# Stick-breaking attention layer: values projected for two pairs of heads with the tokens on the partitions

## The chip, the cores and the metric

The kernel runs on one core of one Trainium2 chip. The metric is the device time of one execution in microseconds, from the first to the last instruction of the program and what lies around them.

## The reference

One layer of a trunk with stick-breaking attention: 2048 tokens, model width 1024, 16 heads of 64, then a SwiGLU feed-forward with 2816 hidden channels. All is float32; the kernel splits operands of most products into a high and a low part and adds three products.

```python
h = modulate(rms_norm(x, norm_g[0]), sh_m, sc_m)
q, k, v = (h @ w_qkv) split, 16 heads of 64
z = q @ k.T / 8                       # per head, keys before the query only
rest = reversed cumulative sum over keys of softplus(z)
a = exp(z - rest)
y = (a @ v) @ w_o
x = x + gt_m * rms_norm(y, norm_g[1])
h = modulate(rms_norm(x, norm_g[2]), sh_f, sc_f)
x = x + gt_f * rms_norm((silu(g) * u) @ w_out, norm_g[3])      # g, u = h @ w_in
```

## The kernel before, in words

**Stages.** First the norm and the modulation of the tokens (four blocks of 512, b = 0 to 3), then attention with the projections woven in, then the output projection (tiles y), the feed-forward (tiles s, then o<-b,ol). The TensorE, ScalarE, VectorE and GpSimd queues run in the order in which the program was written; the order on SP, which issues every transfer, is set by the scheduler. A transfer waits on one of eight semaphores that are used in turn, so at most eight are under way.

**Projections.** Heads go in pairs, p = 0 to 7. A step (p, b) of `project` makes keys, queries and values of one pair for one block of tokens; the steps (0, 0) and (1, 0) are made at the start, in `products`. A product is 8 slices, one for each 128 input channels; a slice is three matmuls of 128x512 (`mm3`, L196 to L198) with the weights stationary and the tokens moving. All three products, t = 1 (keys), 0 (queries) and 2 (values), come out with channels on the partitions. Keys and queries are split into two parts (`split`, L499, L500) and taken by DMA into kt and qt. Values are copied to vT by ScalarE (L539), and after two empty slices (`VGAP`) turned by four transposes of 128x128 into the bank vt (L545), from where ScalarE (L549) and VectorE (L550) write the two parts of the tile v. A step is 3 x 8 + 2 = 26 slices. Normalised tokens are kept in DRAM as h_s and come back for each step in four tiles ht of 1 MB; there are five buffers of ht.

**Attention.** A unit is (p, head e, query block qb, key block sc); it has four slots, one for each 128 queries. In a slot the program writes: scores z (two matmuls, L597), two sigmoids on ScalarE (L614, L616), a scan on VectorE (L631, or L626 on the diagonal), a product on GpSimd (L638), four transposes t (L648), the split of t into aT (ScalarE L658, VectorE L664), and the product with the values o (two matmuls, L676). Later stages belong to earlier slots: transposes are five or six slots behind the scores, products with values nine. Pair p has 80 slots: 8, 16, 24 and 32 for its query blocks 0 to 3.

**The order around the change.** In each slot `project_to` writes projection slices up to a number that grows by a constant rate with the slots done:

```python
AHEAD = 3 * KC + 6
RATE = (sum(SLICES) - AHEAD) / (NPAIR * (48 + 32 * DIAG_WEIGHT) - 24 - 8 * DIAG_WEIGHT)
project_to(AHEAD - max(0, EAGER - 1 - s) + weight * RATE)
```

which is 1.343 slices a slot (a slot on the diagonal counts 0.8). Ahead of a block's first score `project_to` writes whatever its step still lacks. When all 780 slices are written, the first part of the output projection (`lead_in`: L1092 and L1100 on VectorE, then `out_projection`) fills the slots of the last query block.

Of the kernel before, what the change touches and what calls it, by code (L numbers as in the profile page):

```python
# [41 lines left out]
SLICES = [0, 0] + [3 * KC + VGAP] * (NPAIR * NB - 2)  # L42


AHEAD = 3 * KC + 6
DIAG_WEIGHT = 0.8
RATE = (sum(SLICES) - AHEAD) / (NPAIR * (48 + 32 * DIAG_WEIGHT) - 24 - 8 * DIAG_WEIGHT)
# [4 lines left out]
    "ht": 5, "whl": 4, "qt": 3, "kt": 7, "v": 7, "aT": 4, "qkn": 2, "wraw": 2,  # L52
# [40 lines left out]
    2: [(0, 6), (2, 0), (2, 2), (2, 4), (2, 6)],  # L93
    3: [(0, 4), (0, 7), (2, 2), (2, 4), (2, 6)],
# [10 lines left out]
PLACES = [("ht", 64), ("qt", 0), ("v", 0), ("kt", 0), ("whl", 0), ("aT", 0), ("wraw", 0), ("qkn", 0), ("tmp", 0), ("a", 0)]  # L105
# [19 lines left out]
def hybrid_trunk_kernel(  # L125
# [12 lines left out]
    wqkv: bass.AP,  # L138
# [32 lines left out]
    v_park = dram.tile([P, 4, 2, 2, HD], F32, name="v_park")  # L171
# [266 lines left out]
    waiting = []  # L438

    def unpark():  # L440
# [14 lines left out]
        nc.sync.dma_start(f32(v), v_park)  # L455
        keys[p, b], queries[p, b], values[p, b] = kt, qt, v

    def project(at):
# [10 lines left out]
        def product(t):  # L469
            if begun:  # L470
                if at == 0 and t != 2:
                    first_norm(1, 2 + (t == 0))
# [4 lines left out]
            for k in range(KC):
                if t == 1:
                    if p == 0:
                        first_norm(b, NORM_IN_KEYS[b].get(k, KC))  # L480
                    if k in (3, 5) and waiting:
                        waiting.pop(0)()
# [4 lines left out]
                if ahead and k == 0:  # L487
                    load_weights(p + 1, t)
                if ahead and k == 6:
                    split_weights(p + 1, t)  # L490
                mm3(acc, (w[0][:, k], w[1][:, k]), (h[k][:, 0], h[k][:, 1]), k == 0, k == KC - 1)
# [49 lines left out]
        def values_turn():  # L541
            pool, ptag = (zps, "z") if early else (accps, "acc")
            pt = pool.tile([P, 4, 2, HD], F32, name=f"vt{p}_{b}", tag=ptag)
            for i in range(4):
# [3 lines left out]
            v = att.tile([P, 4, 2, 2, HD], F32R, name=f"v{p}_{b}", tag="v", bufs=BUFS["v"])  # L548
            nc.scalar.copy(v[:, :, :, 0], pt)  # L549
            nc.vector.tensor_tensor(v[:, :, :, 1], pt, f32(v[:, :, :, 0]), op=ALU.subtract)  # L550
            if parked:
                nc.sync.dma_start(v_park, f32(v))
            else:
                values[p, b] = v

        if early:
            waiting.append(values_turn)
            return
        for _ in range(VGAP):
            yield  # L560
        values_turn()
# [1229 lines left out]
```

## Time and profile before

| what | value |
|---|---|
| time, median of 3 runs | 2834.68 us (2834.43 to 2834.89) |
| span of the profiled execution | 2832.3 us |
| TensorE (PE) busy | 2795.9 us, 99% |
| VectorE (DVE) busy | 2032.2 us, 72% |
| ScalarE (ACT) busy | 1631.9 us, 58% |
| GpSimd (POOL) busy | 1270.2 us, 45% |
| mean granted clock of TensorE | 0.997 |
| moved by DMA | 521 MB, mean 184 GB/s |

No other time of the profiled execution is given than its span; the median of the runs is 2.4 us above it. Busy time of TensorE counts matmuls that overlap, so that a busy share of 99% doesn't mean the engine at its peak: what a matmul costs is the distance from its start to the next one's.

### The profile page before, as it was taken

The numbers are of one execution on the slowest core, as the hardware profiler recorded it, in microseconds if no ns is written. First come the engines' busy times: TensorE is split into PE (matmuls) and PEld (weight loads), VectorE is DVE, ScalarE is ACT, GpSimd is POOL, SyncE is SP. The second block draws the span as 40 slices with busy tenths as digits, with TensorE's granted clock in tenths as the row PEclk, the third lists the DMA queues.
The fourth block names the chain that finished last, engine by engine and source line by source line (L and its number), as shares of the span: only waits on it lengthen the run. The fifth ranks groups of instructions, "written<-read, shape, count | busy, mean of one in ns | idle before, by whom it ended". The sixth has DMA issues, their size and how long they took to land.

```text
span 2832.3 us, 41825 instructions
## 1 busy us (share of the span) xinstructions
PE 2795.9 (99%) x13817; PEld 2333.2 (82%) x13817; DVE 2032.2 (72%) x2847; ACT 1631.9 (58%) x3277; POOL 1270.2 (45%) x2024
## 2 busy tenths in 40 slices
PE   9899999999999999999999999999999999999998
PEld 7688888888888888887888888888888888888887
DVE  7788888889889888889866766555785665133376
ACT  6787778788777878777655533333433333322243
POOL 1565666666566655656410222221222222544454
PEclk9999999999999999999999999999999999999999
DMA  9874556656665644556289644334463335545575
GB/s 374 303 217 152 187 168 215 223 184 218 198 202 199 205 129 162 194 156 209 95 297 312 203 140 151 123 99 159 133 188 100 110 108 164 192 141 154 181 226 188
DMA packets 240652, 521.06 MB, mean 184 GB/s; under 512 B 22577, under 2 KB 108593, under 8 KB 223538
## 3 DMA queue, kind: packets, MB, share of 16 engines
q1 hardware_dynamic: 240434, 518.38, 56.4%
q8 instruction: 109, 1.79, 0.3%
q14 instruction: 109, 0.89, 0.1%
HBM read 351.04 MB, written 118.49 MB: 166 GB/s over the span
## 4 chain that ended last, share of the span: by engine, by line
PE 89%; DVE 5%; DMA 2%; ACT 2%; issue 1%; SPq 0%; POOL 0%; DVEq 0%; POOLq 0%; ACTq 0%
PE s L196 10%; PE s L198 10%; PE s L197 10%; PE z L597 8%; PE o L676 8%; PE t L648 8%; PE pj L196 5%; PE pj L198 5%; PE pj L197 5%; PE o L196 5%; PE o L197 5%; PE o L198 5%; PE y L198 1%; PE y L196 1%; PE y L197 1%
## 5 line engine op out<-in xcount | busy, mean ns | idle before, releaser
L638 POOL TENSOR_TENSOR a<-a,w 128x512 f32<-128x512 f32 (+3 forms) x640 | 621.9, 972 | 222.2 <-DVE w L631 133.5
L631 DVE TENSOR_TENSOR_SCAN w<-z,c,begin 128x512 f32<-128x512 f32 x384 | 488.9, 1278 | 80.9 <-ACT z L616 61.2
L196 PE MATMUL s<-r,l 128*128 128x512 f32 x1232 | 481.5, 391 | 0.9 <-ACT p L1466 0.8
L198 PE MATMUL s<-r,l 128*128 128x512 f32 x1232 | 479.8, 389 | 0.0
L197 PE MATMUL s<-r,l 128*128 128x512 f32 x1232 | 479.6, 389 | 0.0
L614 ACT ACTIVATE a<-z 128x512 f32<-128x512 f32 (+3 forms) x640 | 346.9, 542 | 165.0 <-PE z L597 131.8
L676 PE MATMUL o<-aT,v 128*128 128x512 f32 (+3 forms) x1280 | 384.8, 382 | 0.0
L664 DVE TENSOR_TENSOR aT<-t,aT 128x512 fp32r<-128x512 f32 (+3 forms) x640 | 359.2, 595 | 23.1 <-ACT aT L658 22.7
L597 PE MATMUL z<-kt,qt 128*128 128x512 f32 (+3 forms) x1280 | 364.1, 366 | 1.7 <-DVE w L626 1.7
L658 ACT CAST aT<-t 128x512 fp32r<-128x512 f32 (+3 forms) x640 | 314.3, 533 | 74.8 <-PE t L648 64.7
L616 ACT ACTIVATE z<-z 128x512 f32<-128x512 f32 (+3 forms) x640 | 345.2, 539 | 0.0
L1530 POOL TENSOR_TENSOR one<-p,p 128x512 f32<-128x512 f32 x44 | 70.9, 1612 | 574.0 <-issue 303.6
L648 PE MATMUL t<-begin,a 128*128 128x128 f32 x2176 | 296.0, 274 | 17.9 <-DVE aT L664 17.0
L648 PEld LDWEIGHTS t<-begin,a 128*128 128x128 f32 x2176 | 255.5, 141 | 68.5 <-DVE aT L664 20.4
L196 PE MATMUL pj<-ht,w 128*128 128x512 f32 x768 | 308.6, 402 | 0.0
L198 PE MATMUL pj<-ht,w 128*128 128x512 f32 x768 | 302.8, 394 | 0.0
L197 PE MATMUL pj<-ht,w 128*128 128x512 f32 x768 | 302.1, 393 | 0.3 <-DVE ht L397 0.3
L196 PEld LDWEIGHTS s<-r,l 128*128 128x128 f32 x1232 | 231.3, 188 | 50.4 <-ACT p L1466 1.7
L198 PEld LDWEIGHTS s<-r,l 128*128 128x128 f32 x1232 | 231.3, 188 | 48.3 <-DVE l L1384 0.4
L197 PEld LDWEIGHTS s<-r,l 128*128 128x128 f32 x1232 | 231.3, 188 | 48.2 <-issue 0.5
L597 PEld LDWEIGHTS z<-kt,qt 128*128 128x128 f32 x1280 | 230.8, 189 | 39.6 <-DVE w L626 2.3
L626 DVE TENSOR_TENSOR_SCAN w<-z,begin 128x128 f32<-128x128 f32 (+3 forms) x256 | 208.6, 818 | 70.7 <-ACT z L616 58.0
(180 smaller groups left out, 4869.8 us busy)
## 6 DMA issues: line engine op xcount, KB each, us to landing
ht<-h_s SPq DMA_DIRECT2D x108, 1024.0 KB, 8.1
wi<-in_win SPq DMA_DIRECT2D x86, 512.0 KB, 4.0
qt<-qn SPq DMA_DIRECT2D x124, 256.0 KB, 4.8
ol_qt<-act_s SPq DMA_DIRECT2D x56, 512.0 KB, 3.6
act_s<-S SPq DMA_DIRECT2D x66, 256.0 KB, 4.1
br<-in_wout SPq DMA_DIRECT2D x66, 256.0 KB, 3.5
h_s<-ht SPq DMA_DIRECT2D x16, 1024.0 KB, 11.1
o_s<-os SPq DMA_DIRECT2D x128, 128.0 KB, 2.6
```

What stands on the lines that cost most here:

```text
L196: nc.tensor.matmul(acc, lhs[0], rhs[0], start=first, stop=False, **kw)
L197: nc.tensor.matmul(acc, lhs[0], rhs[1], start=False, stop=False, **kw)
L198: nc.tensor.matmul(acc, lhs[1], rhs[0], start=False, stop=last, **kw)
L597: nc.tensor.matmul(z[:, :n], q[:, e, part, r * P : (r + 1) * P], k[:, e, :n], start=part == 0, stop=part == 1,)
L614: nc.scalar.activation(a[:, :n], z[:, :n], AF.Sigmoid, scale=QK_SCALE)
L616: nc.scalar.activation(z[:, :n], z[:, :n], AF.Sigmoid, scale=-QK_SCALE)
L631: nc.vector.tensor_tensor_scan(rest[:, rev], left[:, rev], begin[:, :BT][:, rev], initial=carries[r], op0=ALU.mult, op1=ALU.bypass,)
L638: nc.gpsimd.tensor_tensor(a[:, :n], a[:, :n], rest[:, 1 : n + 1], op=ALU.mult)
L648: nc.tensor.transpose(pt[:, rb * P : (rb + 1) * P], weighed[i, rb][:, j * P : (j + 1) * P], ident)
L658: nc.scalar.copy(hl[:, 0, t0:], pt[:, t0:])
L664: nc.vector.tensor_tensor(hl[:, 1, t0:], pt[:, t0:], f32(hl[:, 0, t0:]), op=ALU.subtract)
L676: nc.tensor.matmul(acc[:, t0:], lhs, hl[:, part, t0:], start=sc == qb and j == 0 and part == 0, stop=sc == 0 and j == 3 and part == 1,)
```

## The change

Values of two pairs of heads (a group) are projected at once, and the other way round: a slice of the values is six matmuls of 128x256 (`value_product`) with 128 tokens stationary and 256 value channels moving, for two of the four runs of 128 tokens in a block. So a product of values, 8 slices, is half a block of tokens for two pairs, and comes out with tokens on the partitions; vT, vt and their transposes are gone. The two parts are written by ScalarE and VectorE to a tile vn, stored to DRAM as v_s, two transfers a product, and loaded as v by one transfer of 512 KB at the end of each step. Group g (pairs 2g and 2g + 1) is projected in the steps of pair 2g - 1 (first half of the tokens) and 2g (second half); pair 0 makes both halves of group 0, and pair 7 makes no values. A step has thus 34 slices for pair 0 (and for (2, 0)), 26 for pairs 1 to 6, 18 for pair 7; the sum is 780 as before. The buffers whl (4) become wkq (2) and wv (2). The pace is no longer constant: `pace` follows the upper hull of what each block needs, plus two slices, so that it falls in steps.

```diff
+def value_halves(p, b):
+    if p == NPAIR - 1 or (p, b) == PARKED:
+        return []
+    if p == 0 or (p, b) == (2, PARKED[1]):
+        return [0, 1]
+    return [p % 2 ^ 1]
+def value_group(p):
+    return (p + 1) // 2
+def slices_of(p, b):
+    return 2 * KC + KC * len(value_halves(p, b)) + VGAP
-AHEAD = 3 * KC + 6
+AHEAD = 4 * KC + 6
-RATE = (sum(SLICES) - AHEAD) / (NPAIR * (48 + 32 * DIAG_WEIGHT) - 24 - 8 * DIAG_WEIGHT)
+MARGIN = 2
+def needs():
+    weight = 0.0
+    for p in range(NPAIR):
+        for b in range(NB):
+            at = STEPS.index((p, b)) if (p, b) != PARKED else STEPS.index((p, 1)) - 1
+            yield weight, sum(SLICES[: at + 1]) + 1 + MARGIN
+            weight += 8 * (b + DIAG_WEIGHT)
...
-    "ht": 5, "whl": 4, "qt": 3, "kt": 7, "v": 7, "aT": 4, "qkn": 2, "wraw": 2,
+    "ht": 5, "wkq": 2, "wv": 2, "qt": 3, "kt": 7, "v": 7, "aT": 4, "qkn": 2, "wraw": 2,
...
-    2: [(0, 6), (2, 0), (2, 2), (2, 4), (2, 6)],
-    3: [(0, 4), (0, 7), (2, 2), (2, 4), (2, 6)],
+    2: [(0, 6), (2, 2), (3, 2), (3, 4), (3, 6)],
+    3: [(0, 4), (0, 7), (3, 2), (3, 4), (3, 6)],
...
+    def value_product(acc, g, h, half, k):
+        for i in range(2):
+            ts = slice((2 * half + i) * P, (2 * half + i + 1) * P)
+            mm3(
+                acc[:, i * 2 * P : (i + 1) * 2 * P], (h[k][:, 0, ts], h[k][:, 1, ts]),
+                weights["v", g, k], k == 0 and i == 0, k == KC - 1, skip_group_check=True,
+            )
...
-        acc = yield from product(2)
-        tag = "w" if early else "tmp"
-        vT = att.tile([P, BT], F32, name=f"vT{p}_{b}", tag=tag, bufs=BUFS[tag])
-        nc.scalar.copy(vT, acc)
...
-                nc.tensor.transpose(
-                    pt[:, i].rearrange("p e d -> p (e d)"), vT[:, i * P : (i + 1) * P], ident
...
-            nc.scalar.copy(v[:, :, :, 0], pt)
-            nc.vector.tensor_tensor(v[:, :, :, 1], pt, f32(v[:, :, :, 0]), op=ALU.subtract)
...
+        for half in halves_of_v:
+            acc = yield from product(2 + half)
+            acc = acc.rearrange("p (n d) -> p n d", d=HD)
+            vn = att.tile([P, 2, 2, 2, 2, HD], F32R, name=f"vn{p}_{b}_{half}", tag="qkn", bufs=BUFS["qkn"])
+            to = vn.rearrange("p i q e a d -> p (i q e) a d")
+            nc.scalar.copy(to[:, :, 0], acc)
+            nc.vector.tensor_tensor(to[:, :, 1], acc, f32(to[:, :, 0]), op=ALU.subtract)
+            for pair in range(2):
+                nc.sync.dma_start(
+                    v_s[2 * value_group(p) + pair, b][:, 2 * half : 2 * half + 2], f32(vn[:, :, pair])
+                )
         for _ in range(VGAP):
             yield
-        values_turn()
+        v = att.tile([P, 4, 2, 2, HD], F32R, name=f"v{p}_{b}", tag="v", bufs=BUFS["v"])
+        nc.sync.dma_start(f32(v), v_s[p, b])
+        values[p, b] = v
...
-                project_to(AHEAD - max(0, EAGER - 1 - s) + weight * RATE)
+                project_to(pace(weight) - max(0, EAGER - 1 - s))
```

In the first two steps the values are made by `products`, eight times four groups of three matmuls of 128x256, and `take_first_values` splits them in eight small copies and eight small subtractions; those of (1, 0) are stored, as before. The weights of the values of a group come in two halves, loaded and split in the steps around the change of pair.

Three places show the order. On TensorE, in step (3, 1), before: the end of the values. The names are z and o for scores and products with values, vt for the turned values, pj for projections.

```order
L676 MATMUL o2_0_3_6784<-aT55_0_7054,v2_0_4255 128x512 x2
L597 MATMUL z57_1_7106<-kt2_2_4993,qt2_3_5748 128x512 x2
L545 MATMUL vt3_1_7109<-begin_62,vT3_1_7062 128x128 x4
L196 MATMUL pj3_2_1_7125<-ht3_2_0_7117,w3_1_5525 128x512
L197 MATMUL pj3_2_1_7125<-ht3_2_0_7117,w3_1_5525 128x512
L198 MATMUL pj3_2_1_7125<-ht3_2_0_7117,w3_1_5525 128x512
```

And now, the first slice of the values of that step:

```order
L782 MATMUL o2_0_3_7276<-aT54_2_7491,v2_1_5456 128x512 x2
L703 MATMUL z56_3_7551<-kt2_3_6227,qt2_3_6395 128x512 x2
L248 MATMUL pj3_1_2_7562<-wv2_0_6649,ht3_1_0_7217 128x256
L249 MATMUL pj3_1_2_7562<-wv2_0_6649,ht3_1_0_7217 128x256
L250 MATMUL pj3_1_2_7562<-wv2_0_6649,ht3_1_0_7217 128x256
L248 MATMUL pj3_1_2_7562<-wv2_0_6649,ht3_1_0_7217 128x256
L249 MATMUL pj3_1_2_7562<-wv2_0_6649,ht3_1_0_7217 128x256
L250 MATMUL pj3_1_2_7562<-wv2_0_6649,ht3_1_0_7217 128x256
```

A slice of the values has six matmuls of half the width, and the four transposes at the end of a step are gone.

On TensorE in pair 7, query block 2 (unit 148), between the scores of two slots, before:

```order
L597 MATMUL z148_1_16933<-kt7_0_15238,qt7_2_16542 128x512 x2
L196 MATMUL pj7_3_1_16692<-ht7_3_3_16686,w7_1_14641 128x512
L197 MATMUL pj7_3_1_16692<-ht7_3_3_16686,w7_1_14641 128x512
L198 MATMUL pj7_3_1_16692<-ht7_3_3_16686,w7_1_14641 128x512
L196 MATMUL pj7_3_0_16949<-ht7_3_0_16680,w7_0_14806 128x512
L197 MATMUL pj7_3_0_16949<-ht7_3_0_16680,w7_0_14806 128x512
L198 MATMUL pj7_3_0_16949<-ht7_3_0_16680,w7_0_14806 128x512
L676 MATMUL o7_0_2_16930<-aT146_1_16891,v7_2_16677 128x384 x2
L597 MATMUL z148_2_16968<-kt7_0_15238,qt7_2_16542 128x512 x2
```

and now:

```order
L703 MATMUL z148_1_17684<-kt7_0_16139,qt7_2_17306 128x512 x2
L248 MATMUL pj7_3_0_17638<-ht7_3_1_17357,w7_0_15708 128x512
L249 MATMUL pj7_3_0_17638<-ht7_3_1_17357,w7_0_15708 128x512
L250 MATMUL pj7_3_0_17638<-ht7_3_1_17357,w7_0_15708 128x512
L782 MATMUL o7_0_2_17681<-aT146_1_17642,v7_2_17353 128x384 x2
L703 MATMUL z148_2_17705<-kt7_0_16139,qt7_2_17306 128x512 x2
```

One slice stands here in place of two. Counted over the whole order, the slices between the first score of one query block and that of the next are, for block 2 and 3 of pair 6 and blocks 0, 1 and 2 of pair 7: before 28, 38, 7, 22, 23; now 24, 28, 6, 14, 12. Ahead of the first score of all they were 66 and are 74; in blocks 0 to 3 of pair 0 they were 15, 21, 29, 37 and are 17, 24, 32, 41.

On SP, around the loads of ht for step (3, 3), before:

```order
L229 DMA aw3_0_6_7661<-in_ada_w 128x1024
L532 DMA qt3_2_7451<-qn3_2_7448 64x1024 x4
L415 DMA ht3_3_1_7678<-h_s3_86 128x2048
L415 DMA ht3_3_2_7680<-h_s3_86 128x2048
L415 DMA ht3_3_3_7682<-h_s3_86 128x2048
L684 DMA o_s3_90<-os2_1_3_7617 64x512 x2
```

and now:

```order
L629 DMA qt3_2_8140<-qn3_2_8137 64x1024 x4
L1245 DMA wo_s0_121<-wos0_5_8125 128x1024
L790 DMA o_s0_117<-os3_0_0_8259 64x512 x2
L1238 DMA wor0_6_8360<-in_wo 128x512
L493 DMA ht3_3_1_8375<-h_s3_116 128x2048
L644 DMA v_s4_2_99<-vn3_2_0_8320 128x2x256
L644 DMA v_s5_2_103<-vn3_2_0_8320 128x2x256
L790 DMA o_s0_117<-os3_1_0_8364 64x512 x2
L493 DMA ht3_3_2_8377<-h_s3_116 128x2048
L493 DMA ht3_3_3_8379<-h_s3_116 128x2048
```

The last two tiles of tokens now stand behind the stores of the values (which wait for VectorE) and behind a store of o that waits for ScalarE.

## Rows read from the trace of the kernel before

**Rows 1.** The page: span, and busy time of each engine.
```profile
span 2832.3 us, 41825 instructions
PE 2795.9 (99%) x13817; PEld 2333.2 (82%) x13817; DVE 2032.2 (72%) x2847; ACT 1631.9 (58%) x3277; POOL 1270.2 (45%) x2024
```
**Rows 2.** The page: the chain that ended last, by engine.
```profile
PE 89%; DVE 5%; DMA 2%; ACT 2%; issue 1%; SPq 0%; POOL 0%; DVEq 0%; POOLq 0%; ACTq 0%
```
**Rows 3.** Busy time by stretch, cut at first scores of blocks named in the prediction.
```profile
core 0: us, PE busy (x) PEld busy (x) DVE busy (x) ACT busy (x) POOL busy (x), PEclk, DMA share, GB/s
77.60:99.00 21.40, 19.09 (x97) 15.46 (x96) 15.11 (x30) 15.12 (x32) 7.26 (x17) 0.92 0.99 343
99.00:141.10 42.10, 35.33 (x183) 28.72 (x182) 33.10 (x42) 31.81 (x70) 27.98 (x47) 0.96 0.73 262
141.10:1110.80 969.70, 964.24 (x5326) 819.00 (x5325) 837.90 (x1089) 766.61 (x1616) 619.69 (x1285) 1.00 0.60 192
...
1110.80:1158.40 47.60, 47.60 (x265) 40.65 (x263) 40.80 (x54) 40.04 (x83) 35.07 (x68) 1.00 0.60 204
1158.40:1225.20 66.80, 66.74 (x364) 56.45 (x363) 56.71 (x70) 51.21 (x104) 38.47 (x89) 1.00 0.39 115
1225.20:1240.30 15.10, 15.10 (x90) 13.01 (x89) 12.15 (x18) 11.05 (x27) 6.82 (x18) 1.00 0.79 299
1240.30:1274.70 34.40, 33.01 (x181) 27.76 (x180) 30.20 (x41) 26.05 (x58) 18.50 (x41) 1.00 0.53 146
1274.70:1321.60 46.90, 44.74 (x250) 37.76 (x248) 41.58 (x55) 36.92 (x79) 27.93 (x62) 1.00 0.73 244
1321.60:1383.70 62.10, 59.40 (x328) 49.96 (x328) 57.93 (x73) 51.07 (x108) 38.88 (x87) 1.00 0.16 58
```
**Rows 4.** Timeline of TensorE, end of the program: start us, length us, instruction.
```profile
2811.68 0.39 PE L197 MATMUL o<-b,ol_qt 128*128 128x512 f32 x1
...
2816.44 0.39 PE L197 MATMUL o<-b,ol_aT 128*128 128x512 f32 x1
2816.67 0.39 PE L198 MATMUL o<-b,ol_aT 128*128 128x512 f32 x1
2816.90 0.28 PE L196 MATMUL o<-b,ol_qt 128*128 128x256 f32 x1
2817.01 0.28 PE L197 MATMUL o<-b,ol_qt 128*128 128x256 f32 x1
2817.13 0.28 PE L198 MATMUL o<-b,ol_qt 128*128 128x256 f32 x1
2817.25 0.28 PE L196 MATMUL o<-b,ol_qt 128*128 128x256 f32 x1
```
**Rows 5.** Timeline of TensorE in attention: two scores of 256 columns.
```profile
101.85 0.40 PE L597 MATMUL z<-kt,qt 128*128 128x256 f32 x2
102.08 0.40 PE L196 MATMUL pj<-ht,w 128*128 128x512 f32 x1
```
**Rows 6.** Timeline of TensorE: the transposes of one step's values.
```profile
600.09 0.60 PE L545 MATMUL vt<-begin,vT 128*128 128x128 f32 x4
600.45 0.48 PE L196 MATMUL pj<-ht,w 128*128 128x512 f32 x1
600.76 0.39 PE L197 MATMUL pj<-ht,w 128*128 128x512 f32 x1
```
**Rows 7.** Groups by line, attention: busy us, mean ns, idle before and its releaser.
```profile
L545 PE MATMUL vt<-begin,vT 128*128 128x128 f32 x128 | 19.4, 274 | 0.9 <-ACT vT L539 0.9
...
L539 ACT COPY vT<-pj 128x512 f32<-128x512 f32 x32 | 19.1, 596 | 6.5 <-PE pj L198 6.0 <-ACT z L616 0.4
```
**Rows 8.** Timelines of VectorE, TensorE and SP around the loads of xc.
```profile
106.25 1.85 DVE L384 SCALAR_TENSOR_TENSOR xc<-xc,g_eff,xv 128x512 f32<-128x512 f32 x1 [3.87 <-DMA xc<-in_xt]
...
109.90 0.55 PE L648 MATMUL t<-begin,a 128*128 128x128 f32 x3 [3.75 <-DVE aT L664]
...
94.92 2.44 SPq L331 DMA_DIRECT2D xc<-in_xt  x4
```
**Rows 9.** DMA issues: KB each, median us from issue to landing.
```profile
ht<-h_s SPq DMA_DIRECT2D x108, 1024.0 KB, 8.1
...
v_park<-v SPq DMA_DIRECT2D x1, 512.0 KB, 11.0
```

More of the change, by code (lines that the diff above doesn't have):

```diff
@@ L170, in hybrid_trunk_kernel @@
     k_park = dram.tile([P, 2, BT], F32, name="k_park")
-    v_park = dram.tile([P, 4, 2, 2, HD], F32, name="v_park")
+    v_s = {
+        (p, b): dram.tile([P, 4, 2, 2, HD], F32, name=f"v_s{p}_{b}")
+        for p in range(NPAIR) for b in range(NB) if (p, b) != EARLY[0]
+    }
     h_s = [dram.tile([P, KC, 2, BT], F32, name=f"h_s{b}") for b in range(NB)]
@@ L486, in product @@
                     first_norm(nb, NORM_AT[nb].index((t, k)))
[L487 to L491, printed above, removed]
+                ready_weights(t, k)
+                if t < 2:
+                    w = weights[p, t]
+                    mm3(acc, (w[0][:, k], w[1][:, k]), (h[k][:, 0], h[k][:, 1]), k == 0, k == KC - 1)
+                else:
+                    value_product(acc, value_group(p), h, t - 2, k)
                 slice_at[0] = k
@@ L559, in project, with take_first_values @@
         for _ in range(VGAP):
             yield
-        values_turn()
+        v = att.tile([P, 4, 2, 2, HD], F32R, name=f"v{p}_{b}", tag="v", bufs=BUFS["v"])
+        nc.sync.dma_start(f32(v), v_s[p, b])
+        values[p, b] = v
+    def take_first_values(half):
+        acc = first_acc["v", half].rearrange("p (i q e d) -> p i q e d", q=2, e=2, d=HD)
+        for pair in range(2):
+            if half == 0:
+                first_v.append(
+                    att.tile([P, 4, 2, 2, HD], F32R, name=f"v{pair}_0", tag="v", bufs=BUFS["v"])
+                )
+            to = first_v[pair][:, 2 * half : 2 * half + 2]
+            for i in range(2):
+                nc.scalar.copy(to[:, i, :, 0], acc[:, i, pair])
+                nc.vector.tensor_tensor(to[:, i, :, 1], acc[:, i, pair], f32(to[:, i, :, 0]), op=ALU.subtract)
+        if half == 1:
+            values[EARLY[0]] = first_v[0]
+            nc.sync.dma_start(v_s[PARKED], f32(first_v[1]))
@@ L762, in weights_low, with products @@
             nc.vector.tensor_tensor(lo[:, ks], raw[:, ks], f32(hi[:, ks]), op=ALU.subtract)
-    def products(p, m, *ts):
-        for t in ts or (1, 0, 2):
+    value_split = {}
+    def products(p, m):
+        for t in (1, 0):
             w = weights[p, t]
@@ L770, in products @@
             )
+        if p == 1:
+            for half in range(2):
+                value_product(first_acc["v", half], 0, first_h, half, m)
     def turn_x(m):
@@ L817, in hybrid_trunk_kernel @@
     x_load(0, 3)
-    pairs = [[(p, t) for t in (1, 0, 2)] for p in range(2)]
+    pairs = [[(0, 1), (0, 0)], [(1, 1), (1, 0), "v"]]
     row_load(0)
@@ L855, in hybrid_trunk_kernel @@
     row_done(0)
-    first_acc = {(0, t): accps.tile([P, BT], F32, name=f"pj0_0_{t}", tag="acc") for t in (1, 0, 2)}
+    first_acc = {
+        of: accps.tile([P, BT], F32, name=f"pj0_0_{n}", tag="acc")
+        for n, of in enumerate([(0, 1), (0, 0), ("v", 0)])
+    }
     weights_high(0, *pairs[0])
@@ L874, in hybrid_trunk_kernel @@
     high(1)
-    for t in (1, 0, 2):
-        first_acc[1, t] = zps.tile([P, BT], F32, name=f"pj1_0_{t}", tag="z")
+    for n, of in enumerate([(1, 1), (1, 0), ("v", 1)]):
+        first_acc[of] = zps.tile([P, BT], F32, name=f"pj1_0_{n}", tag="z")
     products(1, 0)
@@ L1373, in left_split @@
         if j == 0:
-            tag = "whl" if (n, pair) == (0, 0) else "ht"
+            tag = "wv" if (n, pair) == (0, 0) else "ht"
             left_pair[n, pair] = att.tile(
```

144 lines of the change are left out of this document (98 added, 46 removed).

## The prediction

> **What bounds the kernel now.** I read the page first. TensorE is busy for 99% of the span and every other engine for 72% or less [rows 1], and 89% of the chain that ended last is TensorE [rows 2]. So a matmul taken away should pay in full, wherever nothing else is close behind. Whether something is close is read from the stretches [rows 3], which I cut at the first score of query blocks: 77.6 is the first score of all, 99.0 and 141.1 those of blocks 1 and 2 of pair 0; 1110.8, 1158.4, 1225.2, 1240.3, 1274.7 and 1321.6 are blocks 2 and 3 of pair 6 and 0, 1, 2, 3 of pair 7; 1383.7 is the last score. The reader is to see three things. From 141.1 to 1110.8 TensorE idles for 5.5 us in 970. At the start it idles for 2.3 us of 21.4 and 6.8 us of 42.1, at a granted clock of 0.92 and 0.96. At the end VectorE is nearly as busy as TensorE: 30.2 against 33.0 us in block 1 of pair 7, 41.6 against 44.7 in block 2, and 57.9 of 62.1 (93%, its highest share in these rows) in block 3.
>
> The median of the runs is 2834.7 us, 2.4 above the profiled span; I add the terms to the median, as if the 2.4 us stayed.
>
> **Values the other way round: -4.1 us.** The change takes away 32 x 24 = 768 matmuls of 512 columns and adds 1536 of 256. Back to back, with a weight load for each, 512 columns start 0.227 us apart (22 starts from 2811.68 to 2816.67) and 256 columns 0.12 apart (three starts from 2816.90 to 2817.25) [rows 4]. So 174.3 us become 184.3: +10.0. Taken away are also 128 transposes. Four of them and one matmul of 512 lie between 600.09 and 600.76 [rows 6]: 0.67 - 0.227 = 0.44, or 0.11 each: -14.1 in all. Two scores of 256 columns between other matmuls took 0.23 together [rows 5]; with 0.115 each the term would be -11.8, and that is its other end. I take the first, since its rows have the same form, three products in a run.
>
> The Trainium skill, page TensorE: Matmul & The Clock Gate, section Back-to-back issue gap, gives a matmul alone N/2.4 + 2.5 ns, by which splitting one in two would cost 2.5 ns; an estimate from that page is +1.9 in place of +10.0. The rows show 13 ns a split, and the measurement decides.
>
> **Copies: nothing, but cover.** 32 copies vT of 0.6 us leave ScalarE [rows 7]; the subtractions on VectorE stay 32. ScalarE isn't the bound, so this is worth no more than TensorE's waits: 0.9 us before vt [rows 7] and part of the 5.5 us idle in the long stretch. The pace there rises from 1.343 to 1.383 slices a slot, which gives the other engines 3% more time. I take -2, between 0 and -5.
>
> **Slices moved to the start: -3.** Eight more slices stand ahead of the first score, and 2 and 3 more in blocks 0 and 1. TensorE has no room ahead of the first score, so the eight are paid there. In blocks 0 and 1 the added 5 x 0.68 = 3.4 us can lie in its 9.1 us of waits, and shorter waits may spare a fall of the clock: a granted share of 0.92 in 21.4 us, and of 0.96 in 42.1, is 1.7 us lost in each. That bounds the gain by -7. Against it stands the longest wait there. VectorE waits 3.87 us for xc, whose loads were issued at 94.9, and TensorE waits 3.75 us behind it [rows 8]. Now the load of v for (0, 1) stands just ahead of xc on SP, and waits until its own stores have landed, in a stretch in which a store of 512 KB took 11 us [rows 9]. The first use of xc also comes later, by the eight slices. I expect this wait to stay about as it is; its worst is +5.
>
> **Slices taken from the end: +10.** This is the term that decides. From 1110.8 to 1321.6 the order has 34 slices fewer (4, 10, 1, 8, 11): 34 x 0.681 = 23.2 us less for TensorE, and 2.6 us fewer transposes (six steps). All of it is paid earlier, in full. What comes back here is limited by VectorE, whose work stays: the scans and splits of 24 slots. I take for each stretch the larger of TensorE's busy time less its slices over 0.98, and VectorE's busy time over 0.96, between its best share of 93% and 100%. In block 2 of pair 7, VectorE gets some 2 us more, since all slices are written four slots before block 3 and the next part of `lead_in` begins there.
>
> - Pair 6, block 2: 47.6 becomes 45.4 (TensorE 44.5).
> - Pair 6, block 3: 66.8 becomes 60.8 (TensorE 59.6; VectorE 56.7).
> - Pair 7, block 0: 15.1 becomes 14.7.
> - Pair 7, block 1: 34.4 becomes 31.5 (VectorE 30.2, TensorE 27.6).
> - Pair 7, block 2: 46.9 becomes 45.4 (VectorE 43.6, TensorE 37.2).
>
> The sum falls by 13.0 us where TensorE's work falls by 25.8. So 12.8 us of moved work find no room, less the 2 us of VectorE's work that block 3 loses, which is itself near its bound: +10 or so. With VectorE at 100% the five stretches take 192.3 and the term is +5; if blocks 1 and 2 of pair 7 didn't get shorter at all, 202.2, and it is +15.
>
> **More transfers: +2.** SP issues 88 transfers more; DMA has room (0.60 of its share in the long stretch [rows 3]). But SP is in order. At five places a load of ht now stands behind a store of the values or of o. Counted in the order, at 0.227 us a matmul, from the last matmul that the load must await to its own first use there are 6.7 us at the tightest ((3, 3), third tile), then 7.1, 8.5 and 8.7; before, 9.7 was the least. From that the copy or split and the issue take some 3 us, and a load of ht lands in 8.1 us in the median, mostly four at a time [rows 9]. So one or two of these waits show, by 1 to 2 us each; none to +6. The queries of pair 7 now end only five slices ahead of their first score, some 10 us; that lies in stretches that VectorE bounds.
>
> Sum: -4.1 - 2 - 3 + 10 + 2 = +2.9. **Forecast: 2837 us, no difference that can be told** (0.2%, 5.7 us, is about what a measurement of this kernel can tell from no change). The gain on TensorE is real, and the moved slices eat it.
>
> **The rivals.**
>
> *TensorE stays the bound to the end (faster).* VectorE's waits for sigmoids shrink as TensorE gets out of the way, and the end stretches go to VectorE's busy time: +4 in place of +10. With -5 at the start, -4 in the middle, no late loads: -4.1 - 5 - 4 + 4 = -9, 2826 us. For it: in blocks 0 and 1 neither engine is full, so added slices may cost nothing. Against it: VectorE never passed 93%. A case of its own within it is cheap halves, a start every 0.115 us: -7.7 more than I take, 2829 us.
>
> *The end doesn't get shorter (slower).* In blocks 1 and 2 of pair 7 VectorE already idles only while ScalarE or TensorE feed it; if its share stays at 93% or less, both blocks keep their time and the term is +15. With late loads (+4) and nothing gained at the start or in the middle: -4.1 + 15 + 4 - 2 = +13, 2848 us. It decides where VectorE's time over 0.93 passes TensorE's demand, which block 2 is far beyond (46.7 against 37). The clock could add to it: at the start it fell in a stretch where TensorE was busy for 84% [rows 3], and 37 of 45 us is no more.
>
> [...]
>
> *SP becomes the bound at the start.* The load of v holds up xc, and the wait of 3.87 us grows to 9: 2842 us. This is a part of the slower case.
>
> *The change doesn't do what it says.* The order shows that it does: the transposes are gone and the slices moved.
>
> **How the numbers follow.** My forecast, 2829 to 2840, 0.42; the faster rival with its cheap halves 0.26; the slower one with SP 0.32. Ends of the terms: -11.8 to -4.1, -5 to 0, -7 to +5, +5 to +15, 0 to +6. All at once is unlikely; -9 to +14 leaves out 2 in 10: 2826 to 2849 us.
>
> **What would show it.** Right: some 1536 matmuls of 256 columns starting 0.12 us apart in slices; no L545; block 2 of pair 7 from first score to first score 44 to 47 us, with VectorE at 94% or more and TensorE's busy share near 80%; pair 6, block 3 near 61; the stretches in the middle longer by 0.3 to 0.6 us each for their added slices, and no more. Wrong: if block 2 of pair 7 falls below 42 us, VectorE's work was not what I took; if the middle stretches don't grow, the idle there was larger than busy time shows; if TensorE waits for ht by more than 6 us in all, the queue is the story.

## The result, and the profile after

| | before | changed |
|---|---|---|
| median time | 2834.14 us (2832.59 to 2837.78, 14 runs) | 2840.39 us (2837.10 to 2847.19, 14 runs) |
| span of the profiled execution | 2832.3 us | 2837.4 us (time 2839.17) |

The ratio is 1.0022, with a 95% interval of 1.0014 to 1.0030: 6.2 us more by the medians. That is just over the 5.7 us (0.2%) that the prediction took for no difference, and the interval lies above 1, so a small loss can be told. The time lies within the range, but 0.4 us above the stretch (2829 to 2840) that the prediction gave its own forecast. The profiled spans differ by 5.1 us, and that is what the rows below account for; the profiled execution of the changed kernel was 1.2 us faster than its median.

The page of the changed kernel, span, busy time by engine and the chain that ended last, beside [rows 1, 2]:

```profile
span 2837.4 us, 43262 instructions
PE 2791.3 (98%) x14457; PEld 2362.6 (83%) x14457; DVE 2029.1 (72%) x2851; ACT 1616.2 (57%) x3248; POOL 1271.6 (45%) x2023
...
PE 84%; DMA 5%; DVE 5%; issue 2%; ACT 2%; POOL 1%; SPq 0%; DVEq 0%; POOLq 0%; ACTq 0%
```

TensorE has 4.6 us less busy time, and its share of the chain fell from 89% to 84%: DMA has 5% of it, where it had 2%.

Busy time by stretch, cut at the same first scores as [rows 3], which now come at 85.3, 111.0 and 145.8, and 1129.4, 1175.6, 1235.5, 1250.7, 1282.0, 1325.1 and 1388.5 (columns as there):

```profile
85.30:111.00 25.70, 20.52 (x122) 17.55 (x121) 16.40 (x32) 16.17 (x35) 7.84 (x18) 0.93 1.02 349
111.00:145.80 34.80, 34.31 (x231) 31.29 (x230) 31.62 (x42) 28.51 (x63) 24.06 (x42) 1.00 0.71 236
145.80:1129.40 983.60, 974.92 (x5897) 854.51 (x5896) 838.89 (x1093) 758.91 (x1599) 625.34 (x1288) 1.00 0.68 216
1129.40:1175.60 46.20, 45.15 (x273) 39.27 (x271) 40.40 (x52) 38.51 (x80) 32.62 (x67) 1.00 0.63 194
1175.60:1235.50 59.90, 59.42 (x331) 50.46 (x330) 53.78 (x67) 48.60 (x100) 37.78 (x88) 1.00 0.77 254
1235.50:1250.70 15.20, 13.98 (x82) 11.97 (x81) 12.53 (x19) 11.40 (x27) 7.10 (x17) 1.00 0.51 132
1250.70:1282.00 31.30, 28.72 (x154) 24.02 (x154) 28.78 (x40) 24.80 (x56) 18.14 (x41) 0.95 0.78 241
1282.00:1325.10 43.10, 38.07 (x213) 30.93 (x211) 42.00 (x57) 36.31 (x78) 28.77 (x63) 1.00 0.79 249
1325.10:1388.50 63.40, 60.16 (x327) 51.15 (x326) 58.28 (x72) 50.95 (x107) 40.10 (x89) 0.97 0.07 20
```

Two things are to be seen. From block 2 of pair 6 to block 3 of pair 7 the five stretches take 195.7 us where they took 210.8, and VectorE is at 97% in block 2 of pair 7 (42.00 of 43.10). And in blocks 1 and 3 of pair 7 the granted clock is 0.95 and 0.97 where it was 1.00: 1.6 and 1.9 us, if the share missing is time lost.

To see where time was lost, set each first score's shift against the work that TensorE had more by then. That work is counted in the order at the durations of the prediction (0.2268 us for 512 columns, which it rounds to 0.227, 0.120 for 256, 0.11 for a transpose):

| up to | later by, us | TensorE's work added | difference |
|---|---|---|---|
| (0, 0) | +7.7 | +5.6 | +2.1 |
| (0, 1) | +12.0 | +7.2 | +4.8 |
| (0, 2) | +4.7 | +9.0 | -4.3 |
| (1, 0) | +11.4 | +14.0 | -2.6 |
| (6, 2) | +18.6 | +21.1 | -2.5 |
| (7, 3) | +3.5 | -4.0 | +7.5 |
| last score | +4.8 | -4.0 | +8.8 |
| end of the span | +5.1 | -4.0 | +9.1 |

The work moved out of the end is 25.1 us and gave back 15.1: that is the 10 us of the prediction's largest term. It didn't come back evenly: block 3 of pair 6 lost 7.2 us of work and became 7.0 shorter, blocks 1 and 2 of pair 7 lost 13.8 and became 7.0 shorter. In these two, TensorE's waits for the split of aT by VectorE rose by 4.8 us (releaser, us in total, times, longest; before from 1240 to 1322 us, then changed from 1250 to 1326):

```profile
PE t L648 <- DVE aT L664: 2.8, 3, 1.2
```

```profile
PE t L754 <- DVE aT L770: 7.6, 9, 2.2
```

With the 1.6 us of the clock that is 6.4 of the 6.8 us that didn't come back. Block 3 of pair 7 adds 1.3. The beginning has two losses that are undone by (0, 2). Both places were tried.

What TensorE waits for up to (0, 2), and what it waits for from there to the last score (releaser, us in total, times, longest):

```profile
PE xT L452 <- DVE vn L642: 3.8, 1, 3.8
PE pj L248 <- ACT ht L479: 3.0, 1, 3.0
...
PE t L754 <- DVE aT L770: 17.1, 21, 2.2
PE pj L248 <- DMA ht<-h_s: 4.9, 5, 1.7
```

Before, the first two weren't there (the waits behind xc [rows 8] were), t waited 10.3 us for aT, and none of ht was late.

### The profile page after: what moved, and what is told of

It is laid out like the page before. It is cut to its first block, busy times and chain, and to the rows that moved or that the text cites. A ratio compares the mean times of both kernels' runs of the same rounds, so it can differ in the third digit from the quotient of the medians.

```text
span 2837.4 us, 43262 instructions
## 1 busy us (share of the span) xinstructions
PE 2791.3 (98%) x14457; PEld 2362.6 (83%) x14457; DVE 2029.1 (72%) x2851; ACT 1616.2 (57%) x3248; POOL 1271.6 (45%) x2023
## 4 chain that ended last, share of the span: by engine, by line
PE 84%; DMA 5%; DVE 5%; issue 2%; ACT 2%; POOL 1%; SPq 0%; DVEq 0%; POOLq 0%; ACTq 0%
PE s L248 10%; PE s L249 10%; PE s L250 10%; PE o L782 8%; PE z L703 8%; PE t L754 8%; PE pj L248 5%; PE pj L250 5%; PE pj L249 5%; PE o L250 4%; PE o L249 4%; PE o L248 4%; DMA ht<-h_s 2%; PE y L250 1%; PE y L248 1%
## 5 line engine op out<-in xcount | busy, mean ns | idle before, releaser
L1512 DVE TENSOR_TENSOR l<-ls,l 128x512 fp32r<-128x512 f32 x172 | 129.5, 753 | 156.2 <-ACT l L1511 155.9
L782 PEld LDWEIGHTS o<-aT,v 128*128 128x128 f32 x1280 | 212.9, 191 | 21.3 <-issue 1.0
L1543 POOL TENSOR_TENSOR ol_qt<-ol_qt 128x1024 fp32r<-128x1024 f32 x56 | 139.7, 2494 | 194.1 <-ACT ol_qt L1542 175.5
```

Source lines behind the costliest of these rows:

```text
L782: nc.tensor.matmul(acc[:, t0:], lhs, hl[:, part, t0:], start=sc == qb and j == 0 and part == 0, stop=sc == 0 and j == 3 and part == 1,)
```

## The experiments

**Theory.** VectorE bounds the end, so TensorE's work that was taken from there came back in part; the start has two new waits, 3.0 and 3.8 us; loads of ht are late. **Rival.** TensorE bounds the end as it does the rest, and the loss is in the matmuls of 256 columns, in SP's queue or in the middle. Each run is compared with the kernel before on the same chip.

### 1 and 2. The same work left out at the end and in the middle

```diff
-                mm3(acc, (w[0][:, k], w[1][:, k]), (h[k][:, 0], h[k][:, 1]), k == 0, k == KC - 1)
+                if not (p == 7 and b > 1 and (t == 2 and 0 < k < 7 or t == 0 and k in (2, 4))):
+                    mm3(acc, (w[0][:, k], w[1][:, k]), (h[k][:, 0], h[k][:, 1]), k == 0, k == KC - 1)
```

in the kernel before, and the same with p == 4.

> The kernel before, with eight of the 26 slices left out in each of steps (7, 2) and (7, 3) (their matmuls alone: k = 1 to 6 of the values, k = 2 and 4 of the queries; the output lacks these parts). That is 16 x 0.681 = 10.9 us of TensorE's work in the two stretches before blocks 2 and 3 of pair 7. Theory 1 (VectorE bounds the end): only 4 to 6.5 us come back, block 1 goes from 34.4 to 31.5 us or so and block 2 from 46.9 to 44, and VectorE's busy share there rises to 94% or more. Rival (TensorE bounds the end too): 10 to 11 us come back, and the loss of the change lies elsewhere (matmuls of 256 columns, SP, the middle).

> The same 16 slices' matmuls left out of steps (4, 2) and (4, 3) of the kernel before (the output lacks these parts). Both theories: TensorE bounds this stretch, so 10 to 11 us come back. Theory 1 wants it to be clearly more than what the same slices give in pair 7; the rival wants the two to be equal within 2 us.

Measured: 0.9989 (0.9980 to 0.9998) and 0.9981 (0.9973 to 0.9990). By first scores, 4.9 us came back in pair 7 (blocks 1 and 2: 2.5 and 2.4) and 6.6 in pair 4, of 10.9. The first is what the theory said. The second fits neither's 10 to 11 us: in the middle, too, a good third was lost; and the two lie within the 2 us of each other that the rival wanted. Two holes of six slices each were cut there, so the work left out was uneven. Hence the next two.

### 5 and 6. The same work left out evenly

```diff
+                if p == 7 and b > 1:
+                    nc.tensor.matmul(acc, w[0][:, k], h[k][:, 0], start=k == 0, stop=False)
+                    nc.tensor.matmul(acc, w[1][:, k], h[k][:, 0], start=False, stop=k == KC - 1)
+                else:
+                    mm3(acc, (w[0][:, k], w[1][:, k]), (h[k][:, 0], h[k][:, 1]), k == 0, k == KC - 1)
```

and with p == 4.

> The kernel before, with the middle one of the three matmuls of each slice left out in steps (7, 2) and (7, 3): 48 matmuls of 512 columns or 10.9 us of TensorE's work, as in the first experiment, but spread evenly instead of in two holes (the output lacks that product). Theory 1 (VectorE bounds the end): 4 to 6.5 us come back between the first scores of (7, 1) and (7, 3), half of it or so, and the clock may fall there. Rival (TensorE bounds the end): 10 to 11 us.

> The same 48 matmuls left out in steps (4, 2) and (4, 3). Theory 1: in the middle little else is near its bound where no hole of several slots is cut, so 8.5 to 10.9 us come back, clearly more than in pair 7. Rival: TensorE is no more the bound here than there, and the 6.6 us that the holes gave back are all that there is: 6 to 7 us, and about as much in pair 7.

Measured: 0.9971 (0.9959 to 0.9982) and 0.9975 (0.9966 to 0.9985); by first scores 7.6 us in pair 7 (7.0 of them in blocks 1 and 2, over the 4 to 6.5 expected) and 6.8 in pair 4. So the contrast that the theory drew is wrong, and the rival's expectation for the middle holds. Busy time by stretch of both, blocks 1 and 2 of pair 7 in the first:

```profile
1238.50:1268.80 30.30, 28.24 (x160) 23.49 (x159) 28.72 (x41) 25.85 (x58) 18.11 (x41) 1.00 0.52 146
1268.80:1312.80 44.00, 40.30 (x227) 33.23 (x225) 42.28 (x56) 36.58 (x80) 29.10 (x63) 1.00 0.73 243
```

and blocks 1 and 2 of pair 4 in the other:

```profile
755.80:783.30 27.50, 26.16 (x150) 21.66 (x149) 24.88 (x36) 24.42 (x56) 20.12 (x41) 1.00 0.85 289
783.30:832.70 49.40, 47.18 (x261) 38.82 (x259) 44.60 (x60) 39.92 (x84) 37.59 (x71) 1.00 0.69 224
```

VectorE is at 95 and 96% in pair 7, from 88 and 89% [rows 3]; in pair 4 at 90%, from 85 and 86%, with TensorE at 95%. TensorE is the first bound in both places and VectorE stands close behind in both: one matmul of three taken out of a stretch gives back 0.63 to 0.70 of its time. What the change did at the end goes further in the same place: in blocks 1 and 2 of pair 7 run 5 left out 10.2 us and got back 7.0, the change took away 13.8 and got back 7.0 as well, with a fall of the clock that run 5 hadn't. A busy share doesn't settle it alone: in block 3 of pair 6 nearly all came back, with VectorE at 90%.

### 8 and 11. VectorE relieved at the end

In the changed kernel, and as a control in the kernel before:

```diff
-        nc.vector.tensor_tensor(o, parts[:, 0], parts[:, 1], op=ALU.add)
+        eng = nc.gpsimd if b == 0 else nc.vector
+        eng.tensor_tensor(o, parts[:, 0], parts[:, 1], op=ALU.add)
...
-        nc.vector.tensor_tensor(hl[:, 1], o, f32(hl[:, 0]), op=ALU.subtract)
+        eng = nc.gpsimd if b == 0 else nc.vector
+        eng.tensor_tensor(hl[:, 1], o, f32(hl[:, 0]), op=ALU.subtract)
```

> The changed kernel with the additions and subtractions of lead_in (16 on VectorE, 0.5 to 0.6 us each, some 9 us in blocks 1 to 3 of pair 7) on GpSimd. Theory 1: VectorE bounds these blocks, so their 137.8 us (1250.7 to 1388.5) become shorter by 4 to 8 us, mostly in block 2, with the clock falling less. Rival (TensorE or ScalarE bounds them): within 1 us of 137.8, or longer, if GpSimd's own products come late.

> The kernel before with lead_in's additions and subtractions on GpSimd, nothing else: the control of the eighth run. If VectorE is the bound of the end only in the changed kernel, the three stretches behind the first score of (7, 1) (143.4 us) shorten by less than 1.5 us here, against 4.5 us there. If it already shares the bound in the kernel before, as the left-out matmuls say (7.6 of 10.9 us came back), by 1.5 to 3.5 us.

Measured: 1.0004 (0.9995 to 1.0014) for the changed kernel, which had 1.0022 without the edit, and 0.9991 (0.9982 to 1.0000) for the kernel before. Blocks 1 to 3 of pair 7, changed kernel with the edit:

```profile
1251.00:1279.40 28.40, 27.22 (x153) 22.71 (x152) 25.13 (x36) 24.54 (x57) 21.08 (x44) 1.00 0.77 231
1279.40:1321.40 42.00, 37.93 (x212) 31.09 (x212) 36.97 (x48) 36.10 (x78) 36.54 (x72) 1.00 0.81 267
1321.40:1384.20 62.80, 59.28 (x328) 49.81 (x327) 55.66 (x68) 50.73 (x107) 43.78 (x93) 1.00 0.09 28
```

They take 133.2 us instead of 137.8, and 140.3 instead of 143.4 in the control. TensorE's work is the same with and without the edit, so VectorE's was part of the bound in both kernels. The clock is at 1.00 throughout; of the 4.6 us up to 3.5 are the clock's falls that went away with the waits. Without them the changed kernel gained less than the control, so it isn't shown that VectorE bounds it more. Nor was the gain mostly in block 2, as expected: there VectorE lost 5.0 us of work, and the stretch only 1.1. A part of the bound passed to GpSimd, as the rival had warned: it is busy for 36.5 of 42.0 us (28.8 before the edit). TensorE's waits from 1230 to 1390 us in the eighth run, where the changed kernel had 12.0 us for aT and none for GpSimd:

```profile
PE t L754 <- DVE aT L770: 7.4, 9, 1.9
PE t L754 <- POOL a L744: 1.3, 1, 1.3
PE t L754 <- POOL w L717: 1.0, 2, 0.5
```

In block 2 of the control TensorE is busy throughout:

```profile
1273.60:1318.20 44.60, 44.52 (x249) 37.66 (x248) 37.16 (x48) 36.80 (x79) 34.32 (x69) 1.00 0.80 272
```

The profiled span of the eighth run is only 1.6 us below the changed kernel's, since 1451.6 us follow its last score instead of 1448.9. That part varies: it takes 1447.2 to 1450.8 us in the other profiles with the same matmuls in it.

### 7. More for TensorE at the end

```diff
-OUT_BEFORE = 28
+OUT_BEFORE = 36
```

> The changed kernel with OUT_BEFORE = 36 instead of 28: the output projection may begin as soon as all slices of the projections are written, some four slots before block 3 of pair 7, and gives some eight more slices to the slots in which TensorE waits for VectorE. Theory 1: these slices cost little there and are missing behind the last score, so the time falls by 2.5 to 5 us, and the clock doesn't fall in block 3 (1.00 instead of 0.97). Rival (TensorE bounds the end, work moved within it changes nothing): the same time within 1 us, or worse, if the slices wait for their operands at the head of TensorE's queue.

Measured: 1.0028 (1.0017 to 1.0038), no gain. Block 2 of pair 7 takes 45.0 us instead of 43.1, block 3 62.8 instead of 63.4, and what follows the last score 1448.0 instead of 1448.9: together 0.4 us more. (The other 3.5 us of its longer span come earlier, mostly with waits for ht of 7.3 us in all instead of 4.9.) Blocks 2 and 3 of pair 7:

```profile
1285.50:1330.50 45.00, 41.23 (x228) 33.83 (x226) 43.45 (x58) 37.73 (x81) 29.84 (x65) 1.00 0.77 242
1330.50:1393.30 62.80, 60.93 (x337) 51.68 (x336) 57.32 (x71) 49.88 (x107) 38.91 (x87) 1.00 0.10 26
```

The 24 matmuls of the eight slices, 5.4 us, were written there, and the two blocks became 1.3 us longer. The clock didn't fall in block 3, as the theory said, which is worth 1.9; so the slices cost up to 3.2 of their 5.4 us: cheaper than elsewhere, not free. The step that failed is the other one: the same 24 matmuls are missing behind the last score, and only 0.9 us came back. TensorE waits there for 2.7 us behind aT and 0.9 us behind VectorE's yt, two waits that the changed kernel doesn't have. And as VectorE is busy for 1.5 us longer in block 2, and stays at 97%, that block doesn't tell which of the two engines lengthened it.

### 3 and 4. The two new waits at the start

On ScalarE, ahead of TensorE's wait of 3.0 us, the timeline of the changed kernel shows the copies of the first values taking turns with VectorE's subtractions:

```profile
59.89 0.27 ACT L663 CAST v<-pj 128x128 fp32r<-128x128 f32 x1 [0.43 <-DVE v L664]
60.51 0.27 ACT L663 CAST v<-pj 128x128 fp32r<-128x128 f32 x1 [0.36 <-DVE v L664]
61.13 0.27 ACT L663 CAST v<-pj 128x128 fp32r<-128x128 f32 x1 [0.36 <-DVE v L664]
...
64.86 1.94 ACT L479 ACTIVATE ht<-xc,mod 128x512 fp32r<-128x512 f32 x3
```

Third run, all copies of a half first:

```diff
             for i in range(2):
                 nc.scalar.copy(to[:, i, :, 0], acc[:, i, pair])
-                nc.vector.tensor_tensor(to[:, i, :, 1], acc[:, i, pair], f32(to[:, i, :, 0]), op=ALU.subtract)
+        for pair in range(2):
+            to = first_v[pair][:, 2 * half : 2 * half + 2]
+            for i in range(2):
+                nc.vector.tensor_tensor(to[:, i, :, 1], acc[:, i, pair], f32(to[:, i, :, 0]), op=ALU.subtract)
```

Fourth run, other buffers for vn of one step:

```diff
-... name=f"vn{p}_{b}_{half}", tag="qkn", bufs=BUFS["qkn"])
+... name=f"vn{p}_{b}_{half}", tag="v" if (p, b) == (0, 1) else "qkn", bufs=BUFS["v" if (p, b) == (0, 1) else "qkn"])
```

> The changed kernel, in which take_first_values writes all four copies of a half ahead of its four subtractions, so that ScalarE and VectorE don't wait for each other in turn. Theory 1: the wait of TensorE of 3.0 us near 65.6 goes or falls below 1 us, the first score comes at 82 to 83.5 instead of 85.3 us, and the time falls by 2 to 4 us. Rival (the start pays only its added slices): the first score stays at 85 +- 0.5 and the time is the same.

> The changed kernel, with the two tiles vn of step (0, 1) in buffers of v instead of those of qkn, so that the copies of the values don't wait until the transfers from kn and qn have landed. Theory 1: ScalarE's wait of 4.4 us ahead of vn at 97.3 goes, TensorE's wait of 3.84 us ahead of xT at 98.7 with it, first score to first score of blocks 0 and 1 falls from 25.7 to 21.5 to 23 us, and the time by 2 to 4 us; some of it may come back in block 1 as a wait for a buffer of v. Rival: another wait takes its place at once, and the first score of block 2 stays at 145.8 +- 1.

Measured: 1.0034 (1.0021 to 1.0046) and 1.0030 (1.0019 to 1.0042), neither faster than the change alone. Each removed its own wait: the first score comes at 82.7 us in the third run, and the stretch from block 0 to block 1 takes 20.3 us instead of 25.7 in the fourth. But the first score of (0, 2) comes at 145.4 and 143.6 instead of 145.8: 0.4 and 2.2 us are left. One profile of each tells little here: that score comes at 139.8 to 141.8 us in the six profiles with the start of the kernel before, and at 144.4 to 145.8 in the three with the start of the changed kernel (itself, the seventh and the eighth run). TensorE's waits up to 146 us, third run:

```profile
PE xT L452 <- ACT hf L473: 3.0, 1, 3.0
PE xT L452 <- DVE vn L642: 2.7, 1, 2.7
```

and fourth:

```profile
PE pj L248 <- ACT ht L479: 3.0, 1, 3.0
PE t L754 <- DVE aT L770: 2.9, 1, 2.9
```

In each the later waits take back all or much of what the earlier one gave. The third run also shows the clock: at 0.97 and 0.91 ahead of 78 us in the changed kernel, 1.00 in the third run, where it fell after 78 us instead.

### 9 and 10. The load of v later, and all mended

```diff
-        v = att.tile([P, 4, 2, 2, HD], F32R, name=f"v{p}_{b}", tag="v", bufs=BUFS["v"])
-        nc.sync.dma_start(f32(v), v_s[p, b])
-        values[p, b] = v
+        late_v.append((p, b))
+        if closing:
+            load_late_v()
...
                 ready_weights(t, k)
+                if (t, k) == (1, 3):
+                    load_late_v()
```

where `load_late_v` holds the three lines taken out. The ninth run has this and the edit of the eighth, the tenth those of the third and fourth as well.

> The kernel of the eighth run (lead_in on GpSimd), in which the load of v of a step is written only at the fourth slice of the next step, behind that step's four loads of ht, so that SP doesn't hold an ht behind a load of v that waits for its own stores. Theory (the load of v at the head of SP's queue makes the loads of ht late): TensorE's waits for ht, 4.5 to 7.3 us in the runs so far, fall below 2 us, and the time falls by 3 to 5 us against the eighth run. Rival (DMA is simply busy, or the buffers of ht come free too late): the waits for ht stay at 4 us or more, and the time is the same within 1.5 us.

> The ninth kernel with the edits of the third and the fourth as well (copies first, vn of step (0, 1) in buffers of v). Singly, these two gave 0.5 and 2.2 us at the first score of block 2, since another wait took the place of the one removed. Theory (they guard the same stretch, and only both together free it): the first score of (0, 2) comes at 140 to 142 us instead of 145.8 and the time falls by 3 to 5 us more, to 2827 to 2831, below the kernel before. Rival (the start is bound by its transfers, DMA at 1.0 of its share to 112 us): 143.5 us or later, and 0 to 2 us less time.

Measured: 1.0013 (1.0005 to 1.0022) and 0.9997 (0.9988 to 1.0006). So the ninth run is no faster than the eighth (1.0004), against its theory. The tenth is 3.4 us faster than the ninth by the medians, within the 3 to 5 us expected, but with 2833.8 us not below the kernel before. TensorE's waits for ht from 146 to 1384 us, ninth and then tenth run:

```profile
PE pj L248 <- DMA ht<-h_s: 2.5, 4, 1.5
```

```profile
PE pj L248 <- DMA ht<-h_s: 4.9, 5, 1.7
```

They were 6.6 us in the eighth, and 4.5 to 7.3 in the changed kernel and the third, fourth, seventh and eighth runs, which have the same order there. The place that the theory was made from, in the changed kernel (SP's timeline; the third load of ht stands behind one of v, for which SP waits 4.4 us until its stores have landed):

```profile
496.22 1.01 SPq L493 DMA_DIRECT2D ht<-h_s  x1
501.72 0.33 SPq L650 DMA_DIRECT2D v<-v_s  x1
502.14 0.38 SPq L493 DMA_DIRECT2D ht<-h_s  x1
```

and in the ninth run:

```profile
495.54 1.53 SPq L493 DMA_DIRECT2D ht<-h_s  x2
500.80 0.33 SPq L281 DMA_DIRECT2D wvr<-in_wv  x1
501.23 0.38 SPq L661 DMA_DIRECT2D v<-v_s  x1
501.70 0.38 SPq L493 DMA_DIRECT2D ht<-h_s  x1
```

Here SP stands at a load of weights instead, and the load of v still comes ahead of the last ht. So the cause isn't settled: the waits are shorter in one of the two runs and as long as ever in the other. What can be said is that they are paid nearly one for one: from (0, 2) to (6, 2) the changed kernel and the eighth, ninth and tenth runs take 983.6, 985.2, 981.9 and 983.7 us, and less their waits for ht 978.7, 978.6, 979.4 and 978.8.

Both edits at the start together gave 3.9 us at (0, 2), 142.0 instead of 145.8, more than the 0.4 and 2.2 singly, and just at the late end of the 140 to 142 us that the theory wanted; all of it is still there at (1, 0). There the old wait is back, the same as in [rows 8]. VectorE and TensorE in the tenth run:

```profile
108.52 0.75 DVE L462 SCALAR_TENSOR_TENSOR xc<-xc,g_eff,xv 128x512 f32<-128x512 f32 x1 [3.72 <-DMA xc<-in_xt]
...
PE t L768 <- DVE aT L784: 3.4, 1, 3.4
```

In all, the tenth run is level with the kernel before. No version of the change tried here is shown to be faster than it; the least ratio without work left out is the control's of the eleventh run (0.9991), which has the edit of lead_in without the change.

### 12. The first use of xc later

```diff
-    3: [(0, 4), (0, 7), (3, 2), (3, 4), (3, 6)],
+    3: [(0, 7), (2, 2), (3, 2), (3, 4), (3, 6)],
```

> The tenth kernel, in which the first two parts of the norm of block 3 are written three and four slices later (NORM_AT[3] begins with (0, 7), (2, 2) instead of (0, 4), (0, 7)), since there VectorE waits 3.7 us for xc again, and TensorE 3.4 us behind it, as in the kernel before. Theory (that wait is a matter of when xc is first used, and is the last in the stretch): the first score of (0, 2) comes at 137.5 to 140 us instead of 142.0, the clock stays at 1.00 from 103 us on, and the time falls by 2 to 4.5 us, to 2829 to 2832, below the kernel before. Rival (the transfers bound the stretch): another wait of the same size takes its place, 141.5 us or later, and the time stays within 1.5 us.

Measured: 1.0004 (0.9995 to 1.0013), no gain. The first score of (0, 2) comes at 136.9 us, 5.1 earlier, better than expected, and the wait is gone. The next stretch gives it all back, and more: 58.5 us to (0, 3) instead of 51.0. The likely cause is on SP: loads of the next pair's weights now stand behind the load of v (issued at 144.51, at 134.0 in the tenth run), and ScalarE stands still for one of them:

```profile
151.95 1.04 ACT L275 CAST w<-wr 128x1024 fp32r<-128x1024 f32 x1 [6.45 <-DMA wr<-in_wqk]
...
136.90:195.40 58.50, 53.72 (x320) 46.98 (x319) 41.54 (x53) 41.62 (x87) 36.44 (x70) 0.94 0.77 230
```

The second row is that stretch, with the clock at 0.94.

## Why the prediction was right

Right in the time's range and in the mechanism of the term that decides. The size came out larger: +5.1 us by the spans and +6.2 by the medians, where +2.9 was forecast. Of the 2.2 us between the spans and the forecast, 1.3 are block 3 of pair 7 and 0.4 the start. That the middle came out as forecast is luck: there cheaper splits and shorter waits cancelled late loads.

- **Values the other way round, -4.1.** Counted over the whole order at the durations of the prediction it is -4.0. The starts are as close as taken or closer, twelve in a run with 1.30 us from the first to the last, 0.118 apart (changed kernel, TensorE's timeline):

```profile
615.74 0.28 PE L248 MATMUL pj<-wv,ht 128*128 128x256 f32 x1
615.86 0.27 PE L249 MATMUL pj<-wv,ht 128*128 128x256 f32 x1
...
617.04 0.28 PE L250 MATMUL pj<-wv,ht 128*128 128x256 f32 x1
```

  By these rows a split costs 2 x 0.118 - 0.227 = 9 ns for the 13 taken, and the term is -7: up to 3 us of the work counted as added in the table aren't there, and were lost to waits instead. That is still over the 2.5 ns of the Trainium skill (TensorE: Matmul & The Clock Gate, Back-to-back issue gap); an estimate from that figure puts the term at -12. No run timed it by itself.
- **Copies and cover, -2; transfers, +2.** Between (1, 0) and (6, 2) the kernel is longer by 7.2 us, for 7.1 us of added work: the two sum to 0.1, as forecast to 0. But the waits for ht are 4.9 us there, five of them where one or two were expected. Against them stand TensorE's other waits, 2.5 us where they were 5.4, so that the cover gave 2.9; the other 1.9 us fit the cheaper splits (516 of them there at 4 ns less are 2.1). The prediction drew its line at 6 us of waits for ht in all; the profiled execution stays below it, but the seventh and eighth runs, with the same order there, have 7.3 and 6.6.
- **Slices moved to the start, -3.** -4.3 at (0, 2), -2.6 at (1, 0). The size came, but not in the way said: the wait behind xc was to stay, and it is gone, since xc landed 8.7 us after its issue in the median, where it took 11.9 before; why it landed sooner isn't shown. Not foreseen were the two new waits, copies by turns and vn's buffer. So two things that were not expected balance, and the term held by luck as much as by its reasons. It is also no sharper than the 1 or 2 us by which the start varies from profile to profile.
- **Slices taken from the end, +10.** The five stretches were forecast at 45.4, 60.8, 14.7, 31.5 and 45.4 us and took 46.2, 59.9, 15.2, 31.3 and 43.1: 195.7 in all for 197.8. (The lower bound of 192.3, called VectorE at 100%, has TensorE at 100% too; with VectorE alone the five come to 194.7.) The larger of TensorE's and VectorE's demand, each over its best share, was a fair way to price them; VectorE went to 97% in block 2 of pair 7, past the 96% taken. Block 3, for which 2 us of gain were put down, became longer by 1.3, with the clock at 0.97: of lead_in's work on VectorE only 0.5 us left it (3.1 to 2.6), and the fall of the clock wasn't in the sum. The term comes to 10.0 + 1.3 = 11.3. The waits for aT and runs 1, 5, 8 and 11 bear its mechanism out; it isn't shown that VectorE alone is the bound, since in run 8 a good part of its work went away for 1.1 us in block 2. Of the signs, VectorE's 97% came true; block 2 itself fell just below its 44 to 47 us, with TensorE at 88% where some 80% were expected, and the stretches of pairs 3 to 5 changed by -1.1 to +2.5 us where 0.3 to 0.6 were.
- **The rivals.** That the end goes to VectorE's busy time (faster) fell: 15.1 us came back of 25.1, where a term of +4 needs some 19. In block 2 of pair 7 alone it was nearly so, with VectorE busy for 42.0 of 43.1 us; and its cheap halves came about halfway, 0.118 us apart for the 0.120 taken and the 0.115 of that case. That the end doesn't shorten fell too: blocks 1 and 2 of pair 7 shrank by 3.1 and 3.8 us. SP at the start didn't become the bound: no wait behind xc is left.

The sum, -4.0 + 0.1 - 2.6 + 11.3 and 0.3 behind the last score, is the 5.1 us of the spans, for the 2.9 forecast. The medians differ by 1.1 us more, about what the profiled execution was faster than its median; no trace shows where.

## What to carry to other kernels

Adding and removing work on the busiest engine aren't priced alike: in the middle, where TensorE was busy for 99%, 7.1 us of added slices cost 7.2, the late loads included; removed ones gave back 0.6 to 0.7 where a second engine stood at 85 to 90%, and 0.5 where more was taken. Work that is moved into a stretch without idle time is therefore paid nearly in full, and the stretch that it leaves must be priced by the second engine. And a wait that is removed from a crowded stretch is worth only what the next wait leaves: look for that one before expecting the length of the first.

## What the runs showed of the hardware

- The granted clock fell behind pieces in which TensorE stood waiting for VectorE's aT. In the changed kernel it is at 0.50 of full speed (the lower level, 1.2 GHz) from 1274.2 and from 1328.8 us; TensorE was busy for 3.62 of the 6.20 us ahead of the first and 2.12 of the 4.80 us ahead of the second, VectorE for 5.54 and 4.80. This gives the 0.95 and 0.97 of blocks 1 and 3 of pair 7; in runs 5 and 8 both are at 1.00. In run 5 TensorE's busy share in block 1 (28.24 of 30.30 us, 93%) was about that of the changed kernel (92%), so the share of a whole stretch doesn't tell whether it falls.
- Stretches between the same first scores repeat to 0.1 us in the profiles of two kernels, where nothing in them was changed: all 27 from (0, 2) to (7, 1) did so between the kernel before and run 1. Differences of a few tenths in such a stretch are effects, though no median of whole runs would show them. This doesn't hold where transfers decide: between the changed kernel and the eighth run, with the same order there, three stretches in the middle differ by 1.2 to 1.6 us with the waits for ht, and the first score of (0, 2) varies by 2 us.
